# A four-stage trunk on one core: head 0's f and q together in the first stage, and a new order of loads and norms ahead of them

## The chip, the cores and the metric

The kernel runs on one core of a Trainium2 chip. The metric is device time in microseconds (us): the median of several executions of the same program. A separate execution was taken by the hardware profiler, and every row of the profile is from that one.

## The reference

One inference step of a two-layer decoder trunk, in float32, for 1024 prompt tokens and 8 sample tokens (T = 1032 columns), with shared weights:

```python
def hgrn2_mixer(h, s0, w_in, lb, g_norm, w_out):       # layer 0
    q, f, i, z = jnp.split(h @ w_in, [D_MODEL, 2 * D_MODEL, 2 * D_MODEL + D_INNER], axis=-1)
    q = jax.nn.silu(q)                                   # 8 heads of 128
    logf = jnp.logaddexp(jnp.log(lbh), jnp.log1p(-lbh) + jax.nn.log_sigmoid(f))
    k = -jnp.expm1(logf)
    o, S = hgrn2_chunkwise(q, k, i, logf, s0)            # gated linear recurrence
    return (rmsnorm(o, g_norm) * jax.nn.silu(z)) @ w_out, S

def trunk(x, p, ...):
    h = x
    for i in range(DEPTH):                               # DEPTH = 2; layer 1 is a chunked gMLP
        hn = rmsnorm(h, norm_mix[i])
        y = hgrn2_mixer(hn, ...) if i % 2 == 0 else chunk_mlp_mixer(hn, ...)
        h = h + y
        gate = jax.nn.sigmoid(rmsnorm(h, norm_ple[i]) @ w_ple_gate[i])
        h = h + gate * (p[i] @ w_ple_proj[i])            # D_MODEL 1024, p has 256 features
    return rmsnorm(h, norm_final), new_s, new_v
```

## The kernel before

**Tiling.** Features lie on the 128 partitions (D_MODEL is eight blocks, k or j = 0 to 7), tokens on the free axis in three chunks c = 0, 1, 2 of W = 384, 384 and 264 columns. A float32 product is made of three matmuls in a reduced format (`mm3`): each operand is split into a high part (a cast on ScalarE: `bh` or `ph` for activations, `whi` for weights) and a low part (source minus high part: `bl`, `pl`, `wlo`), and TensorE adds hi·hi, lo·hi and hi·lo in PSUM. A projection `proj` of one 128-wide block of weights for one chunk is eight such triples. In the profile's lines these are L228, L229 (needs the low part of the activation) and L230 (needs `wlo`).

**The first stage**, around which the change lies, in the order of TensorE:

1. Twelve matmuls on zeros as warm-up (`zo<-zr`).
2. `pple(0, ..., half 0)`: the first half of layer 0's p @ w_ple_proj, a fill of work while the first norm runs: for every chunk four output blocks m, each two triples; chunk 0, then 1, then 2. ScalarE copies each result out of PSUM (`pple_t`), and it is stored to DRAM.
3. `first_norm(c)` for each chunk, a process that is stepped on by ticks between the pieces of TensorE work. It squares x (`sq`, ScalarE, two blocks at a time), adds the squares in pairs (`sq<-sq`: VectorE for chunk 0, GpSimd for chunks 1 and 2), sums over partitions on TensorE (`pss<-ones,sq`), takes `rms_e` on VectorE and the power −1/2 on GpSimd (`rsq`), spreads that over the partitions by TensorE (`pbc<-ident,rsq`), scales x by it on VectorE (`scalar_tensor_tensor`, called STT below: `xs<-xs,g,pbc`) and splits the result: `bh` on ScalarE, `bl` on VectorE for odd j and on GpSimd for even j. `SQD` and `SDEL` are the ticks that a process waits ahead of its squares, its sum and its broadcast.
4. For each chunk `fk` and then `qq`: the projection of head 0's forget gate (weights `("a", 8)`), then of its query (`("a", 0)`). ScalarE takes sigmoids of the one (`f`, and k into `qk`) and of the other (`sg`), and VectorE makes q = ps·sg (into `qk`).
5. Two blocks of z (weights `("a", 32)`, `("a", 33)`, called z0 and z1 below), while VectorE and ScalarE form mixed tiles of the normed x for the next stage (`mix_x`: `xs<-xs,xs`, then `xzh` and `xzl`).

**What sets the order.** TensorE runs in program order, written by hand. On the other engines a scheduler orders by program order, data and priority: work under `tc.high_priority(offset=PRI)` goes ahead, and `tc.issue_after(x)` keeps an instruction behind x. The accumulators of `pple` and `proj` share three PSUM banks (tag `mm`), those of the sums one. Input and output transfers are issued by SyncE, whose queue holds eight transfers open at a time: each issue waits for the eighth before it.

`norm_proc` serves the first norm (`own=True`: x is scaled in place) and the later norms (`own=False`: into one of four `tmp` buffers), among these the ones ahead of the two gate products (`ps_proj` at 912 us and its like in layer 1), which run beside the last output products (`ps_o`, added to `h` on VectorE).

```python
            split(hh[:, j, :], hl[:, j, :], t[:, :w], V if j % 2 else G)
...
    for c in CH:
        fk(0, r0, wf, c)
        qq(0, r0, wq, c)
```

Of the kernel before, what the change touches and what calls it, by code (L numbers as in the profile page):

```python
# [80 lines left out]
def trunk_kernel(ctx, tc, xT, st, pT, nrm, wina, lbl, gna, wouta, winb, lng, lnb, lngr, lnbr,  # L81
# [27 lines left out]
    with ExitStack() as s:  # L109
        zp = pool(s, "warm")  # L110
        zps = pool(s, "warm_ps", space=PSUM)
        zf = zp.tile([P, 512], F32, name="zf")
# [2 lines left out]
        V.tensor_copy(zr, zf)
        zo = zps.tile([P, 512], F32, name="zo")
        for _ in range(NWARM):
            PE.matmul(zo, zr[:, :P], zr, start=True, stop=True)
# [174 lines left out]
    def norm_proc(sp, ssq, src, gi, hh, hl, c, d, own=False):  # L293
# [6 lines left out]
        w = W[c]  # L300
        for j in range(KT):
            t = src(j) if own else sp.tile([P, 384], F32, name="tmp", bufs=4)
            V.scalar_tensor_tensor(t[:, :w], src(j), g32[:, gi, j:j + 1], pbc[:, :w], ALU.mult, ALU.mult)
# [1440 lines left out]
```

## Time and profile before

| | |
|---|---|
| time, median of 3 runs | 1866.89 us (1864.61 to 1870.77) |
| profiled execution, its own time | 1863.58 us |
| its span, first to last instruction | 1861.6 us |
| mean granted TensorE clock | 0.995 |
| busy: TensorE / VectorE / ScalarE / GpSimd | 98% / 73% / 48% / 22% |
| DMA, mean over the span | 137 GB/s of HBM traffic |
| first stage: warm-up from 2.01 us, first `pple` 7.30, first f 21.92, z0 54.40 | |

A timeline row reads: start and length in us, engine, source line, operation, output and inputs, size on the array, shape, count; in brackets the idle time of the engine ahead of it and what ended that. Matmuls are pipelined: a row of 0.34 us follows its neighbour by 0.17 where nothing is waited for, so rates are taken from starts. PE is TensorE, DVE VectorE, ACT ScalarE, POOL GpSimd.

### The profile page before, as it was taken

The page shows a single profiled execution, that of the slowest core. Times are in us where ns is not written, and L with a number is a line of the kernel's source. Part 1 is how long each engine was busy: PE and PEld are TensorE (multiplying, and loading weights), DVE is VectorE, ACT ScalarE, POOL GpSimd, SP SyncE. Part 2 cuts the span into 40 slices and gives each one's busy share as a digit, 9 for nine tenths or more (in the row PEclk, how much of TensorE's full clock was granted, in tenths as well). Part 3 has the DMA queues.
Part 4 walks back from the last instruction along what each step waited for, and adds up shares of the span by engine and source line. Part 5 has one row for each costly group of instructions (what it writes and reads, how often), then busy time and mean ns, then how long its engine had stood idle before and what let it go on. Part 6 is the DMA issues. An engine that isn't in the chain of part 4 may idle for free.

```text
span 1861.6 us, 37133 instructions
## 1 busy us (share of the span) xinstructions
PE 1822.4 (98%) x14458; PEld 1788.6 (96%) x14458; DVE 1360.5 (73%) x2760; ACT 897.6 (48%) x1905; POOL 402.3 (22%) x407
## 2 busy tenths in 40 slices
PE   8999999999999999999999999999999999999997
PEld 7999999999999998999999999999999999999997
DVE  7766888889888875867756755577778877877744
ACT  7533366556656655344444544434443435444342
POOL 4000011111111110000323233354444552000222
PEclk9999999999999999999999999999999999999999
DMA  6233344345444355853244343323334546953223
GB/s 220 79 112 106 112 127 128 108 152 182 149 130 140 117 176 185 278 184 96 87 145 140 101 136 92 95 79 119 129 117 143 172 129 215 305 179 104 72 92 114
DMA packets 164560, 258.11 MB, mean 139 GB/s; under 512 B 16096, under 2 KB 136864, under 8 KB 163360
## 3 DMA queue, kind: packets, MB, share of 16 engines
q1 hardware_dynamic: 164384, 255.74, 43.5%
q8 instruction: 113, 1.85, 0.4%
q14 instruction: 63, 0.52, 0.1%
HBM read 182.88 MB, written 72.80 MB: 137 GB/s over the span
## 4 chain that ended last, share of the span: by engine, by line
PE 80%; DVE 10%; DMA 5%; issue 2%; POOL 1%; ACT 1%; SPq 0%; DVEq 0%; ACTq 0%; POOLq 0%
PE ps_proj L228 19%; PE ps_proj L230 18%; PE ps_proj L229 18%; PE ps_d L228 2%; PE ps_o L228 2%; PE ps_d L230 2%; PE ps_d L229 2%; PE ps_o L229 2%; PE ps_o L230 2%; DVE wlo L150 1%; PE psp L1526 1%; DMA vb<-vd 1%; PE pt_o L899 1%; PE pt_g L1408 1%; PE pC L807 1%
## 5 line engine op out<-in xcount | busy, mean ns | idle before, releaser
L228 PE MATMUL ps_proj<-bh,whi 128*128 128x264 f32 (+1 forms) x2248 | 719.2, 320 | 4.3 <-ACT u L493 1.3
L229 PE MATMUL ps_proj<-bl,whi 128*128 128x264 f32 (+1 forms) x2248 | 700.8, 312 | 5.4 <-DVE bl L224 2.7
L230 PE MATMUL ps_proj<-bh,wlo 128*128 128x264 f32 (+1 forms) x2248 | 700.9, 312 | 1.2 <-DVE wlo L150 1.2
L228 PEld LDWEIGHTS ps_proj<-bh,whi 128*128 128x128 f32 x2248 | 423.6, 188 | 12.3 <-issue 3.3
L229 PEld LDWEIGHTS ps_proj<-bl,whi 128*128 128x128 f32 x2248 | 424.1, 189 | 8.9 <-DVE bl L224 5.4
L230 PEld LDWEIGHTS ps_proj<-bh,wlo 128*128 128x128 f32 x2248 | 422.6, 188 | 2.1 <-DVE wlo L150 2.1
L150 DVE TENSOR_TENSOR wlo<-wstg,whi 128x1024 fp32r<-128x1024 f32 x148 | 183.7, 1241 | 109.4 <-ACT whi L149 109.1
L149 ACT CAST whi<-wstg 128x1024 fp32r<-128x1024 f32 x148 | 155.2, 1049 | 150.0 <-PE ps_proj L229 125.0
L149 ACT CAST shi<-ssum 128x512 fp32r<-128x512 f32 x152 | 94.1, 621 | 187.3 <-PE ps_proj L229 90.1
L150 DVE TENSOR_TENSOR slo<-ssum,shi 128x512 fp32r<-128x512 f32 x152 | 113.9, 751 | 9.2 <-ACT shi L149 8.8
L237 POOL TENSOR_TENSOR rsq<-rms_e,mhalf 128x3 f32<-128x3 f32 x15 | 17.8, 1187 | 368.1 <-DVE rms_e L282 368.1
L857 DVE TENSOR_TENSOR qk<-qk,t 128x384 f32<-128x384 f32 (+1 forms) x144 | 77.2, 540 | 12.0 <-PE pC L807 11.3
L228 PE MATMUL ps_proj<-xmh,shi 128*128 128x384 f32 x244 | 83.0, 340 | 1.9 <-ACT xmh L223 1.7
L229 PE MATMUL ps_proj<-xml,shi 128*128 128x384 f32 x244 | 81.9, 336 | 0.7 <-DVE xml L224 0.7
L230 PE MATMUL ps_proj<-xmh,slo 128*128 128x384 f32 x244 | 81.7, 335 | 0.0
L228 PE MATMUL ps_o<-bh,whi 128*128 128x384 f32 (+1 forms) x232 | 73.4, 316 | 0.0
L230 PE MATMUL ps_o<-bh,wlo 128*128 128x384 f32 (+1 forms) x232 | 72.7, 313 | 0.0
L229 PE MATMUL ps_o<-bl,whi 128*128 128x384 f32 (+1 forms) x232 | 72.7, 313 | 0.0
L1535 POOL TENSOR_TENSOR s<-s,u 128x384 f32<-128x384 f32 (+1 forms) x48 | 54.1, 1127 | 70.9 <-DVE s L1529 70.3
L1274 DVE TENSOR_TENSOR tmp<-tmp,pj 128x384 f32<-128x384 f32 (+1 forms) x48 | 25.6, 534 | 55.9 <-ACT tmp L1273 52.0
L237 POOL TENSOR_TENSOR rsq<-ss_e,mhalf 128x3 f32<-128x3 f32 (+2 forms) x32 | 28.4, 889 | 145.7 <-DVE ss_e L893 145.7
L264 POOL TENSOR_TENSOR ssq<-ssq,tmp 128x384 f32<-128x384 f32 (+1 forms) x36 | 34.3, 951 | 108.1 <-ACT tmp L263 108.1
(376 smaller groups left out, 4135.8 us busy)
## 6 DMA issues: line engine op xcount, KB each, us to landing
wstg<-in_wina SPq DMA_DIRECT2D x48, 512.0 KB, 3.8
wstg<-in_winb SPq DMA_DIRECT2D x48, 512.0 KB, 4.0
pj<-ppd SPq DMA_DIRECT2D x16, 516.0 KB, 4.9
S<-in_st SPq DMA_DIRECT2D x16, 512.0 KB, 5.4
vb<-vd SPq DMA_DIRECT2D x16, 512.0 KB, 4.8
out_so_s<-S SPq DMA_DIRECT2D x16, 512.0 KB, 3.5
wstg<-in_wouta SPq DMA_DIRECT2D x16, 512.0 KB, 4.2
wstg<-in_wgate SPq DMA_DIRECT2D x16, 512.0 KB, 3.7
```

The costliest lines, as they stand in the source:

```text
L149: A.copy(hi, src)
L150: V.tensor_tensor(lo, src, hi.bitcast(F32), ALU.subtract)
L228: PE.matmul(ps, wh, xh, start=first, stop=False, skip_group_check=more)
L229: PE.matmul(ps, wh, xl, start=False, stop=False, skip_group_check=more)
L230: PE.matmul(ps, wl, xh, start=False, stop=last, skip_group_check=more)
L237: G.tensor_tensor(y, e, mhalf[:, :n], ALU.pow)
L264: eng.tensor_tensor(ssq, ssq, sq[:, :w], ALU.add)
L807: PE.matmul(out(slice(row, row + kt.shape[1])), kt, qt, start=True, stop=True)
L857: V.tensor_tensor(lev, lev, t2.rearrange("p two (n o) -> p two n o", o=1).broadcast_to([P, 2, n, lv]), ALU.mult)
L899: PE.transpose(pt[:, m, :], on[:, m * P:(m + 1) * P], ident)
L1274: V.tensor_tensor(gt[:, :w], gt[:, :w], pj[:, OFF[c]:OFF[c] + w], ALU.mult)
L1535: G.tensor_tensor(s[:, :w], s[:, :w], us[mm, c][:, :w], ALU.mult)
```

## The change

- The warm-up's operand shrinks from 128x512 to 128x128; its moving side is one column read 512 times.
- Loads: the first weights (`("p", 0, 0)`) come in pieces of 256 and 768 columns, chunk 0's p in two halves between them; x of chunk 0 follows at once; p of chunks 1 and 2, each followed by the weights of f or q, stands behind chunk 0's x and the constants. q's weights are split during the fill (`load(2)` at i = 5).
- First norm: all low parts on VectorE, STT and low part alternating (STT j behind low part j − 2), at high priority; for chunks 1 and 2 no pair additions on GpSimd, TensorE sums eight rows in place of four (96 matmuls in place of 48 for each of them). `SQD` and `SDEL` are new. The `pple` copies of this half go to high priority.
- `proj2`: for chunks 0 and 1 f and q run k by k in two banks; chunk 2 stays f, then q.
- The later norms get `high_priority(offset=0)` around STT and split.

```diff
-SQD = (0, 6, 12)
+SQD = (0, 10, 14)
-SDEL = ((6, 3), (6, 2), (4, 2))
+SDEL = ((6, 2), (4, 1), (4, 1))
...
-        zr = zp.tile([P, 512], F32R, name="zr")
+        zr = zp.tile([P, P], F32R, name="zr")
-            PE.matmul(zo, zr[:, :P], zr, start=True, stop=True)
+            PE.matmul(zo, zr, zr[:, 0:1].broadcast_to([P, 512]), start=True, stop=True)
...
+        lows = []
         for j in range(KT):
             t = src(j) if own else sp.tile([P, 384], F32, name="tmp", bufs=4)
-            V.scalar_tensor_tensor(t[:, :w], src(j), g32[:, gi, j:j + 1], pbc[:, :w], ALU.mult, ALU.mult)
-            split(hh[:, j, :], hl[:, j, :], t[:, :w], V if j % 2 else G)
+            with tc.high_priority(offset=PRI if own else 0):
+                with tc.issue_after(lows[j - 2].ins) if own and j > 1 else ExitStack():
+                    V.scalar_tensor_tensor(t[:, :w], src(j), g32[:, gi, j:j + 1], pbc[:, :w], ALU.mult, ALU.mult)
+                split(hh[:, j, :], hl[:, j, :], t[:, :w], V if j % 2 or own else G)
+            lows.append(last["lo"])
...
-                with tc.high_priority(offset=PRI if l else 0):
+                with tc.high_priority(offset=0 if half and not l else PRI):
                     last["pple"] = A.copy(t, ps[:, :W[c]])
...
-    load(0)
+    loaded[0] = [t.rearrange("p k t -> p (k t)")[:, :1024] for t in (hh[2], hl[2])]
+    first_weights(0, 2 * P)
-    load_p(sp, 0, 0, ph, pl)
-    load_p(sp, 0, 1, ph, pl)
+    load_p(sp, 0, 0, ph, pl, single=True)
+    first_weights(2 * P, 1024)
     load_x(0)
...
+    load_p(sp, 0, 1, ph, pl)
+    fetch_weights(1)
     load_p(sp, 0, 2, ph, pl)
+    fetch_weights(2)
     load_x(1)
-    fetch_weights(1)
     load_x(2)
-    fetch_weights(2)
...
-            eng.tensor_tensor(sq[:, j, :], sq[:, j, :], sq[:, j + 1, :], ALU.add)
+            if not c:
+                V.tensor_tensor(sq[:, j, :], sq[:, j, :], sq[:, j + 1, :], ALU.add)
-    ... norm_proc(sp, [sq[:, j, :] for j in range(0, KT, 2)], ...
+    ... norm_proc(sp, [sq[:, j, :] for j in range(0, KT, 1 if c else 2)], ...
...
+    def proj2(w1, w2, c):
+        both = [(wt, pp.tile([P, 512], F32, name="ps_proj", tag="mm", bufs=3)) for wt in (w1, w2)]
+        for k in range(KT):
+            for (wh, wl), ps in both:
+                mm3(ps[:, :W[c]], blk(wh, k), blk(wl, k), hh[c][:, k, :], hl[c][:, k, :], k == 0, k == KT - 1)
+            if k in (1, 3, 5):
+                tk.tick()
+        return [ps for _, ps in both]
...
-        if i == 8:
-            with tc.issue_after(last["pple"].ins):
-                load(1)
+        if i == 5:
+            load(2)
...
     for c in CH:
-        fk(0, r0, wf, c)
-        qq(0, r0, wq, c)
+        pf, pq = proj2(wf, wq, c) if c < 2 else (None, None)
+        fk(0, r0, wf, c, pf)
+        qq(0, r0, wq, c, pq)
```

How instructions move is shown at three places. The number after a name's underscore tells one use of a buffer from another; `ps_proj_504` is chunk 0's f before, `ps_proj_563` its q, `ps_proj_436` and `ps_proj_437` the same two after, `ps_proj_644` chunk 1's f before; `xs1`, `bh1`, `bl1` are chunk 1's, `xs2`, `bl2` chunk 2's.

First, ScalarE where chunk 0's f and q leave PSUM, before:

```order
L223 CAST bh1_137<-xs1_155 128x384 x2
L605 ACT_TABLE_LOAD
L605 ACTIVATE f_529<-ps_proj_504 128x384
L606 ACTIVATE qk_530<-ps_proj_504 128x384
L607 ACTIVATE f_529<-f_529,lb_182 128x384
L618 ACTIVATE sg_588<-ps_proj_563 128x384
L608 ACTIVATE qk_530<-qk_530,lb_182 128x384
L223 CAST bh1_137<-xs1_155 128x384 x6
```

and after:

```order
L223 CAST bh1_137<-xs1_155 128x384 x2
L632 ACT_TABLE_LOAD
L632 ACTIVATE f_620<-ps_proj_436 128x384
L223 CAST bh1_137<-xs1_155 128x384 x2
L633 ACTIVATE qk_621<-ps_proj_436 128x384
L645 ACTIVATE sg_626<-ps_proj_437 128x384
L634 ACTIVATE f_620<-f_620,lb_180 128x384
L223 CAST bh1_137<-xs1_155 128x384
```

Two casts of chunk 1 now stand between the two sigmoids that read f's bank (L605 and L606 before are L632 and L633 after).

Second, VectorE in the norms of chunks 1 and 2, before:

```order
L303 SCALAR_TENSOR_TENSOR xs1_155<-xs1_155,g32_72,pbc_535 128x384 x4
L619 TENSOR_TENSOR qk_530<-ps_proj_563,sg_588 128x384
L282 TENSOR_SCALAR rms_e_640<-pss_591 128x3
L644 TENSOR_SCALAR gn16_813<-gn16_813 128x2
L425 TENSOR_TENSOR xs0_154<-xs1_155,xs0_154 128x384
L224 TENSOR_TENSOR bl1_140<-xs1_155,bh1_137 128x384
```

and after:

```order
L306 SCALAR_TENSOR_TENSOR xs1_155<-xs1_155,g32_72,pbc_580 128x384
L224 TENSOR_TENSOR bl1_140<-xs1_155,bh1_137 128x384
L646 TENSOR_TENSOR qk_621<-ps_proj_437,sg_626 128x384
L224 TENSOR_TENSOR bl1_140<-xs1_155,bh1_137 128x384
L282 TENSOR_SCALAR rms_e_740<-pss_643 128x3
L435 TENSOR_TENSOR xs1_155<-xs1_155 128x384 x2
L306 SCALAR_TENSOR_TENSOR xs2_156<-xs2_156,g32_72,pbc_756 128x264 x2
```

Chunk 2's `rms_e` stood ahead of chunk 1's last three low parts (of VectorE's four) and stands behind all eight now.

Third, VectorE in the norm ahead of layer 0's gate product (`tmp`, `bh0` and `bl0` are its chunk 0; `h2_6` and `h2_7` are the last additions of the output products), before:

```order
L303 SCALAR_TENSOR_TENSOR tmp_12321<-h0_3_10573,g32_72,pbc_12305 128x384
L224 TENSOR_TENSOR bl0_12231<-tmp_12313,bh0_12228 128x384
L1150 TENSOR_TENSOR h2_6_10592<-h2_6_10592,ps_o_12345 128x264
L282 TENSOR_SCALAR rms_e_12383<-pss_12370 128x3
L303 SCALAR_TENSOR_TENSOR tmp_12325<-h0_4_10574,g32_72,pbc_12305 128x384
L150 TENSOR_TENSOR wlo_12167<-wstg_12164,whi_12166 128x1024
L224 TENSOR_TENSOR bl0_12231<-tmp_12321,bh0_12228 128x384
L303 SCALAR_TENSOR_TENSOR tmp_12329<-h0_5_10575,g32_72,pbc_12305 128x384
L1150 TENSOR_TENSOR h2_7_10593<-h2_7_10593,ps_o_12391 128x264
```

and after:

```order
L306 SCALAR_TENSOR_TENSOR tmp_12413<-h0_3_10665,g32_72,pbc_12397 128x384
L306 SCALAR_TENSOR_TENSOR tmp_12417<-h0_4_10666,g32_72,pbc_12397 128x384
L1179 TENSOR_TENSOR h2_6_10684<-h2_6_10684,ps_o_12437 128x264
L282 TENSOR_SCALAR rms_e_12475<-pss_12462 128x3
L150 TENSOR_TENSOR wlo_12259<-wstg_12256,whi_12258 128x1024
L306 SCALAR_TENSOR_TENSOR tmp_12421<-h0_5_10667,g32_72,pbc_12397 128x384
L306 SCALAR_TENSOR_TENSOR tmp_12425<-h0_6_10668,g32_72,pbc_12397 128x384
L1179 TENSOR_TENSOR h2_7_10685<-h2_7_10685,ps_o_12483 128x264
L224 TENSOR_TENSOR bl0_12323<-tmp_12405,bh0_12320 128x384
L224 TENSOR_TENSOR bl0_12323<-tmp_12413,bh0_12320 128x384
```

The low parts of blocks 1 and 3 stood ahead of the addition to `h2_7` and stand behind it now. In layer 1's gate norm the same rows move in the same way.

More of the change, by code (lines that the diff above doesn't have):

```diff
@@ L318, in proj, with load_p @@
         return ps
-    def load_p(ap, l, c, ph, pl, behind=None, to=None):
+    def load_p(ap, l, c, ph, pl, behind=None, to=None, single=False):
         stg = ap.tile([P, 2, W[c]], F32, name=f"pstg{c}", bufs=1)
+        if single:
+            ph[c], pl[c] = [ap.tile([P, 2, W[c]], F32R, name=f"p{x}{c}") for x in "hl"]
+            for k in range(2):
+                load_split(ph[c][:, k], pl[c][:, k], pT[l][:, k, OFF[c]:OFF[c] + W[c]], stg[:, k])
+            return
         nc.sync.dma_start(stg, pT[l][:, :, OFF[c]:OFF[c] + W[c]])
@@ L558, in load_x, with first_weights @@
             nc.sync.dma_start(xs[c][:, j:j + 2, :], xT[:, j:j + 2, OFF[c]:OFF[c] + W[c]])
-    load(0)
+    loaded[0] = [t.rearrange("p k t -> p (k t)")[:, :1024] for t in (hh[2], hl[2])]
+    w0stg = wp.tile([P, 1024], F32, name="wstg")
+    def first_weights(a, b):
+        load_split(loaded[0][0][:, a:b], loaded[0][1][:, a:b], wproj[0, 0][:, a:b], w0stg[:, a:b])
     ph, pl = [None] * 3, [None] * 3
-    load_p(sp, 0, 0, ph, pl)
-    load_p(sp, 0, 1, ph, pl)
+    first_weights(0, 2 * P)
+    load_p(sp, 0, 0, ph, pl, single=True)
+    first_weights(2 * P, 1024)
     load_x(0)
@@ L581, in first_norm @@
         sq = sp.tile([P, KT, 384], F32, name="sq0", bufs=2)[:, :, :W[c]]
-        eng = V if c == 0 else G
         for j in range(0, KT, 2):
@@ L586, in first_norm @@
                 A.activation(sq[:, j:j + 2, :], xs[c][:, j:j + 2, :], AF.Square)
-            eng.tensor_tensor(sq[:, j, :], sq[:, j, :], sq[:, j + 1, :], ALU.add)
-        yield from norm_proc(sp, [sq[:, j, :] for j in range(0, KT, 2)], lambda j: xs[c][:, j, :], 0, hh[c], hl[c], c, SDEL[c], True)
+            if not c:
+                V.tensor_tensor(sq[:, j, :], sq[:, j, :], sq[:, j + 1, :], ALU.add)
+        yield from norm_proc(sp, [sq[:, j, :] for j in range(0, KT, 1 if c else 2)], lambda j: xs[c][:, j, :], 0,
+                             hh[c], hl[c], c, SDEL[c], True)
     V.tensor_tensor(lb[:, 1, :], lb[:, 0, :], lb[:, 0, :], ALU.subtract)
@@ L611, in fk, with qq @@
         tk.tick()
-    def qq(h, r, wt, c):
+    def qq(h, r, wt, c, ps=None):
         w = W[c]
-        ps = proj(wt, hh[c], hl[c], c)
+        ps = ps or proj(wt, hh[c], hl[c], c)
         sg = fq.tile([P, 384], F32, name="sg", bufs=2)
@@ L628, in trunk_kernel @@
     for i, _ in enumerate(fill):
-        if i == 8:
-            with tc.issue_after(last["pple"].ins):
-                load(1)
+        if i == 5:
+            load(2)
         tk.tick()
     r0 = new_head()
-    wf, wq = take("a", 8), take("a", 0)
+    wf, wq = take("a", 8), loaded[2]
     for c in CH:
-        fk(0, r0, wf, c)
-        qq(0, r0, wq, c)
+        pf, pq = proj2(wf, wq, c) if c < 2 else (None, None)
+        fk(0, r0, wf, c, pf)
+        if c == 2:
+            take("a", 0)
+        qq(0, r0, wq, c, pq)
     assert not tk.procs
```

6 lines of the change are left out of this document (3 added, 3 removed).

## The prediction

> **What bounds the kernel now.** I read the page's head first, then the busy time by stretches of the stage that the change touches, then what TensorE waited for there (from 0 to 56 us), then the timelines engine by engine.
>
> ```profile
> span 1861.6 us, 37133 instructions
> PE 1822.4 (98%) x14458; PEld 1788.6 (96%) x14458; DVE 1360.5 (73%) x2760; ACT 897.6 (48%) x1905; POOL 402.3 (22%) x407
> ...
> 21.90:31.40 9.50, 6.40 (x40) 4.65 (x31) 8.97 (x10) 6.16 (x13) 9.17 (x8) 1.00 0.84 279
> 31.40:43.80 12.40, 11.02 (x154) 9.79 (x152) 10.94 (x21) 7.53 (x16) 5.35 (x6) 1.00 0.15 46
> 43.80:54.40 10.60, 10.31 (x75) 10.09 (x75) 10.60 (x22) 8.26 (x21) 3.41 (x4) 1.00 0.00 0
> 54.40:77.40 23.00, 22.82 (x147) 22.51 (x146) 20.11 (x37) 12.50 (x27) 0.00 (x0) 1.00 0.34 108
> ...
> PE ps_proj L229 <- POOL bl L224: 2.5, 3, 1.1
> PE zo L118 <- DVE zr L115: 2.0, 1, 2.0
> PE ps_proj L229 <- DVE bl L224: 2.0, 3, 1.1
> PE ps_proj L230 <- DVE wlo L150: 0.5, 2, 0.3
> ```
>
> PE is busy 98% of the span, so the change can win only what PE loses where it reaches. After each stretch stand its length and the busy time of PE, PEld, DVE, ACT and POOL, then PE's granted clock, the DMA share and GB/s. PE is busy 6.40 of 9.50 us while chunk 0's f runs; POOL (9.17) and DVE (8.97) are full there, and the waits are for low parts from either. In the stretch 43.80 to 54.40 DVE is never idle (10.60 of 10.60), and from 54.40 PE runs full. So the limit is the norm's elementwise work, DVE's above all; whatever makes z0 start earlier or later moves everything behind it.
>
> ```profile
> 2.01 5.49 PE L118 MATMUL zo<-zr 128*128 128x512 f32 x12 [2.01 <-DVE zr L115]
> 7.30 0.52 PE L228 MATMUL ps_pple<-ph,whi 128*128 128x384 f32 x1
> ...
> 21.92 0.44 PE L228 MATMUL ps_proj<-bh,whi 128*128 128x384 f32 x1
> 35.77 0.98 PE L279 MATMUL pss<-ones,sq 128*32 128x1 f32 x96
> 36.68 0.44 PE L228 MATMUL ps_proj<-bh,whi 128*128 128x384 f32 x1
> 43.19 0.73 PE L290 MATMUL pbc<-ident,rsq 128*128 128x128 f32 x6
> 43.78 0.42 PE L228 MATMUL ps_proj<-bh,whi 128*128 128x384 f32 x1
> 48.02 0.28 PE L228 MATMUL ps_proj<-bh,whi 128*128 128x264 f32 x1
> 49.11 0.28 PE L228 MATMUL ps_proj<-bh,whi 128*128 128x264 f32 x1
> 49.47 0.28 PE L228 MATMUL ps_proj<-bh,whi 128*128 128x264 f32 x1
> 54.40 0.34 PE L228 MATMUL ps_proj<-bh,whi 128*128 128x384 f32 x1
> 55.08 0.44 PE L230 MATMUL ps_proj<-bh,wlo 128*128 128x384 f32 x1 [0.18 <-DVE wlo L150]
> ```
>
> Prices: chunk 1's q, eight triples, takes 43.78 to 48.02, so 0.53 us a triple of 384 columns (0.52 taken); one of 264 takes 49.11 to 49.47, 0.36. Chunk 2's sum, right behind chunk 0's q, takes 35.77 to 36.68, 0.91; a broadcast 43.19 to 43.78, 0.59. From f's start at 21.92 to 54.40 are 32.48 us: 32 triples of 0.52 and 16 of 0.36 make 22.4, one sum (0.91; chunk 1's is earlier) and two broadcasts 2.1. The other 8.0 are waits, the most that the reordering of f and q can win.
>
> ```profile
> 1.53 0.43 DVE L115 CAST zr<-zf 128x512 fp32r<-128x512 f32 x1
> 18.94 2.71 DVE L303 SCALAR_TENSOR_TENSOR xs<-xs,g,pbc 128x384 f32<-128x384 f32 x5 [3.49 <-PE pbc L290]
> 22.77 2.58 DVE L224 TENSOR_TENSOR bl<-xs,bh 128x384 fp32r<-128x384 f32 x2
> ...
> 44.01 2.08 DVE L303 SCALAR_TENSOR_TENSOR xs<-xs,g,pbc 128x264 f32<-128x264 f32 x5
> 48.82 0.42 DVE L224 TENSOR_TENSOR bl<-xs,bh 128x264 fp32r<-128x264 f32 x1
> 53.82 1.21 DVE L150 TENSOR_TENSOR wlo<-wstg,whi 128x1024 fp32r<-128x1024 f32 x1
> 57.37 2.89 DVE L224 TENSOR_TENSOR xzl<-xs,xzh 128x384 fp32r<-128x384 f32 x6
> ...
> 6.00 0.83 ACT L326 CAST ph<-pstg 128x768 fp32r<-128x768 f32 x1 [0.28 <-DMA pstg<-in_pT]
> 8.45 0.85 ACT L586 ACTIVATE sq<-xs 128x768 f32<-128x768 f32 x1 [0.19 <-DMA xs<-in_xT]
> 9.51 0.85 ACT L586 ACTIVATE sq<-xs 128x768 f32<-128x768 f32 x1 [0.22 <-DMA xs<-in_xT]
> ...
> 33.42 1.28 ACT L605 ACT_TABLE_LOAD   x1
> 34.71 0.49 ACT L605 ACTIVATE f<-ps_proj 128x384 f32<-128x384 f32 x1
> 36.94 2.58 ACT L223 CAST bh<-xs 128x384 fp32r<-128x384 f32 x6
> 15.53 0.85 POOL L237 TENSOR_TENSOR rsq<-rms_e,mhalf 128x3 f32<-128x3 f32 x1 [15.02 <-DVE rms_e L282]
> ```
>
> An STT takes 2.71 / 5 = 0.54. A low part takes 2.89 / 6 = 0.48 where POOL stands still (`xzl`), but 2.58 / 2 = 1.29 at 22.77, while POOL makes low parts itself. The Trainium skill (SBUF — State Buffer, "SBUF: two separate sides") says that VectorE with two SBUF inputs and GpSimd shut each other out of a shared port for a whole instruction; those 1.29 us agree.
>
> **The change part by part.** The walk below carries these prices through the new order.
>
> *Warm-up and first products.* The cast of 512 columns takes 0.43, the memset ahead of it about as much; a quarter of the columns saves at most 0.65. The first weights and p come in pieces, so the first `pple` starts at about 6.7 in place of 7.30 (bounds: 7.3, if the halved p is no earlier, and 6.6). Chunk 0 is eight triples, 4.2: PE is through at 10.9.
>
> *p of chunk 1 behind x of chunk 0.* Two squares that wait for DMA start 1.06 apart, so one such piece (128x768 words) lands in 1.06. With chunk 1's p out of their way, x's four pieces land 1.06 earlier, the last at 10.6 by that pace; constants (mostly two tables of 128x128, 0.4) and p (1.06) follow, 12.0. Ahead of p's cast in ACT's queue stand the last square (0.85), one `pple` copy and the exponential of `lb`, which itself waits for DVE: I put the cast's end at 13.3 (0.83 long) and `pl`, 0.95, at 14.3. q's weights are split in the fill (1.21 on DVE), in the 3.49 in which DVE was idle ahead of 18.94: nothing, or 1.2 later STTs if that idle time goes. The `pple` copies' priority costs nothing: PE waited for no bank, and a copy pushes a square back by less than 0.5. SyncE's queue holds nothing else back: the weights of f and q come behind p, and f starts at 22 us. So PE, which had no wait here, stands still from 10.9 to 13.3 at least and 15.2 at most, if the constants' chain on DVE holds `pl` up: 3.4 taken, of which the earlier start had given 0.6. Behind it in PE's order: four triples (2.1) to 16.4, chunk 0's sum (0.9) to 17.3, four triples to 19.4, the broadcast to 20.0. So STT begins at 20.0 (bounds 18.9, as before, and 20.9) where it began at 18.94. Chunk 2's eight small triples, 2.9, end at 22.9, and f and q begin 1.0 later than f did.
>
> *Low parts on DVE, f and q k by k, chunk 0.* DVE needs 0.54 + 0.48 = 1.02 a block, PE two triples, 1.04: they keep pace as long as POOL touches nothing, and its pair additions are gone. Those cost PE instead one doubled sum, 1.8 (0.9 more for each of chunks 1 and 2). 22.9 + 8.3 + 1.8 + 0.6 = 33.6. Before, q of chunk 0 ended at 35.77: 2.1 won.
>
> *Chunk 1.* q needs a third bank, which is f's of chunk 0 until both its sigmoids are done. f ends at 33.1, the table load takes 1.28, the sigmoid 0.4, and now two casts (2.58 / 6 = 0.43 each) stand ahead of the second sigmoid: 36.1. PE has one triple of f to do, so it waits 2.1 (bounds 1.2, were the table loaded early, and 2.5). Seven blocks follow: to 39.6 with the sum's 1.8, to 41.7 with two more. Chunk 2's `rms_e` now stands behind all of chunk 1's low parts on DVE, so `rsq` (0.85) is done at 42.4 and PE, at its broadcast, waits 0.7 (0 to 1.5). With 0.6 and four blocks: 47.3.
>
> *Chunk 2*, f then q as before. DVE has eight STTs of 2.08 / 5 = 0.42 and eight low parts of 0.42 (before: half of them), and ACT makes the high parts between chunk 1's sigmoids and scalings, 2.6 in all. The last low part comes at 51.0, f ends at 51.4, q eight triples later: 54.3.
>
> *z0* needs `wlo` (1.21) behind some seven mixing steps and low parts of 0.48 on DVE: 51.0 + 3.4 + 1.2 = 55.6, at the worst 56.9. Before, PE's first triple with it was at 55.08. So the end of the stage moves by +0.5 to +1.8; **+1.1** is taken. Everything won by pairing f and q is given back by DVE's sum (8 of 1.02 each for two chunks, 8 × 0.84, the mixing) from a later STT.
>
> *The gate norms.* Here the low parts are pushed back, in two places.
>
> ```profile
> 909.15 0.55 DVE L224 TENSOR_TENSOR bl<-tmp,bh 128x384 fp32r<-128x384 f32 x1
> 912.87 0.43 DVE L1150 TENSOR_TENSOR h<-h,ps_o 128x264 f32<-128x264 f32 x1
> ...
> 912.67 0.34 PE L228 MATMUL ps_proj<-bh,whi 128*128 128x384 f32 x1
> 918.26 0.44 PE L229 MATMUL ps_proj<-bl,whi 128*128 128x384 f32 x1 [0.35 <-DVE bl L224]
> ```
>
> PE starts the gate product at 912.67 and wants block 1's low part 0.53 later. That was made at 909.15; it now stands behind the addition to `h2_7`, which begins at 912.87 because it waits for PE, and behind an STT that waits for a free `tmp`, thus for POOL's low parts: about 915.0, a wait of 1.75. But the product already waited at 918.26 for its last low part, which comes no later than before by more than 0.5, since DVE has the same work to do. So +0.5 each (bounds 0 and 1.75), **+1.0** for two.
>
> Sum: +1.1 + 1.0 = +2.1 on the profiled execution's 1863.58 us. That lies 3.3 below the median of the runs, 1866.89; against the median the forecast is **1869.0**.
>
> **The rivals.** *B, the waits don't bite.* p of chunk 1 is cast as soon as it lands, the second sigmoid and `rms_e` find free slots. PE then goes from 22.9 by 22.4, two doubled sums of 1.8 and two broadcasts to 50.1; DVE's own sum from STT at 20.0 is 8.2 + 8.2 + 6.7 + mixing and `wlo` 6.6, 49.7. z0 began at 54.40 and lost 0.34 to its `wlo`, so that is −4.6; −6.6 if STT also begins at 18. For it: each wait hangs on a queue position worked out by hand. Against: three have to vanish together. 1860 to 1862.
>
> *C, the other side: the gate norms decide.* Two places with three chunks each; if each chunk loses the whole 1.75, that is 10.5: 1877.4. For it: the low parts of all chunks are pushed back alike, with the work of both DVE and POOL between. Against: chunks 1 and 2 have a chunk's product (4 us) of lead. It is slower by over 0.3% from about 0.75 us a chunk, given the stage's +1.1.
>
> *D, the clock.* The new gap of 3.4 us falls where PE has just warmed up. In the trace the granted clock is 1.00 in all four stretches, whose longest wait is 1.1 us, so no gap of this length is shown. If the clock were halved for about as long again, work of 3.4 us would take 1.7 longer at once: 1870.7. For this the Trainium skill (TensorE: Matmul & The Clock Gate, "What's actually happening") speaks: after an idle window of about 3.4 us the array falls to half its clock. By it the sum is +3.8; without it, +2.1.
>
> **How the numbers follow.** A difference of 0.3%, 5.6 us, is about what can be told from no change in this kernel: the band is 1861.3 to 1872.5. Forecast (both terms small): 0.62, from +0 to +5, thus 1867 to 1872. B: 0.18, half of it beyond the band. C: 0.10, nearly all beyond. D: 0.10, inside. Faster 0.10 (half of B and a little), same 0.80, slower 0.10. The range reaches from B's better half to half of C: 1861 to 1875.
>
> **What would show it.** Right: a gap of 2.4 to 4.3 us on PE ahead of chunk 1's first `pple`, ended by `ph` or `pl`; STT at about 20; f and q of chunk 0 without waits to 33.6; a wait of about 2 us ahead of q of chunk 1, ended by the second sigmoid; one for `rsq` ahead of chunk 2's broadcast; z0's `wlo` triple at 55.5 to 56.9; and waits for `bl` early in both gate products. The prediction is wrong if DVE's low parts take 0.5 but the ones on ACT they wait for are late, or if PE works through f and q of all chunks by 50: then z0 moves up by 4 or more. The clock at 11 to 18 us decides D.

## The result: 0.85% slower, and the profile after

The changed kernel takes 1881.87 us (median of 6 runs, 1880.24 to 1886.60) beside 1867.76 for the kernel before on the same chip: ratio 1.0085, 95% interval 1.0066 to 1.0104. The forecast was 1869.0, the range 1861 to 1875. The profiled execution took 1881.57 us, its span:

```profile
span 1879.8 us, 37502 instructions
PE 1829.7 (97%) x14650; PEld 1796.0 (96%) x14650; DVE 1361.7 (72%) x2774; ACT 899.4 (48%) x1907; POOL 380.9 (20%) x387
```

TensorE has 192 rows more, the doubled sums: each of the two has 48 more matmuls, and a matmul of a sum stands in the profile as two rows. What it waited for in the first 60 us, total, times, longest:

```profile
PE pss L279 <- issue: 4.4, 2, 2.6
PE ps_pple L228 <- ACT ph L335: 2.3, 1, 2.3
PE ps_proj L228 <- ACT qk L633: 2.1, 1, 2.1
...
PE ps_pple L229 <- DVE pl L336: 0.6, 1, 0.6
```

The waits of f and q for low parts are gone, as the change intends. The largest entry is one that the prediction has no word for: "issue", time in which the engine waited for nothing that the profile shows, and it lies in the middle of the two long sums. The timeline of TensorE (`bh` and `bl` in rows of `ps_pple` are the first weights, which lie in buffers of that name now):

```profile
14.35 0.44 PE L228 MATMUL ps_pple<-ph,bh 128*128 128x384 f32 x1 [2.31 <-ACT ph L335]
15.34 0.69 PE L229 MATMUL ps_pple<-pl,bh 128*128 128x384 f32 x1 [0.55 <-DVE pl L336]
...
21.90 0.83 PE L290 MATMUL pbc<-ident,rsq 128*128 128x128 f32 x6
25.48 0.34 PE L228 MATMUL ps_proj<-bh,whi 128*128 128x384 f32 x1
30.22 1.34 PE L279 MATMUL pss<-ones,sq 128*32 128x1 f32 x141
33.33 0.61 PE L279 MATMUL pss<-ones,sq 128*32 128x1 f32 x51 [1.77 <-issue]
...
43.17 0.44 PE L228 MATMUL ps_proj<-bh,whi 128*128 128x384 f32 x1 [2.07 <-ACT qk L633]
44.97 1.53 PE L279 MATMUL pss<-ones,sq 128*32 128x1 f32 x163
49.08 0.59 PE L279 MATMUL pss<-ones,sq 128*32 128x1 f32 x29 [2.58 <-issue]
67.73 0.44 PE L230 MATMUL ps_proj<-bh,wlo 128*128 128x384 f32 x1 [0.61 <-DVE wlo L150]
```

A sum of 192 rows breaks off after 141, the next after 163. And z0's first triple with its `wlo`, at 55.08 before, stands at 67.73: +12.65 us, so most of the loss is made in this stage. The busy time by stretches (after the five engines stand the granted clock, the DMA share and GB/s) shows what each gap costs besides itself:

```profile
11.90:14.90 3.00, 0.58 (x2) 0.19 (x1) 2.07 (x9) 2.50 (x5) 0.00 (x0) 0.99 1.04 399
...
14.82:18.23 3.41, 2.89 (x9) 2.89 (x10) 2.31 (x3) 1.61 (x3) 0.00 (x0) 0.50 1.05 375
18.23:35.30 17.07, 15.09 (x366) 14.15 (x365) 10.12 (x19) 11.97 (x24) 1.71 (x2) 1.00 0.84 275
35.30:38.72 3.42, 3.42 (x15) 3.42 (x14) 0.51 (x1) 0.00 (x0) 0.00 (x0) 0.50 0.01 2
38.72:48.95 10.23, 5.71 (x186) 5.04 (x184) 9.18 (x20) 7.32 (x14) 0.00 (x0) 1.00 0.01 2
48.95:55.78 6.83, 6.70 (x50) 6.69 (x51) 1.95 (x6) 0.33 (x1) 1.09 (x1) 0.50 0.01 2
55.78:67.70 11.92, 10.85 (x72) 9.90 (x71) 11.21 (x27) 9.13 (x22) 0.00 (x0) 1.00 0.01 1
```

Three times, behind the gap ahead of chunk 1's p and behind each broken sum, the granted clock is exactly 0.50, for 3.41, 3.42 and 6.83 us. TensorE is busy for 13.0 us of these, and at half clock half of that is lost: 6.5 us. The Trainium skill (TensorE: Matmul & The Clock Gate, "What's actually happening") gives just two clocks, full and half, and a window of about 3.4 us; the 0.50 and the lengths 3.4 and 6.8 agree.

The spells start 20.48 and 13.65 us apart, six and four times 3.41. So it is in all traces, this one, the one of before and those of the experiments: a spell of half clock that ends before the program does lasts a whole multiple of 3.41 us, and within one trace any two start a whole multiple of 3.41 us apart. The clock is thus set anew in fixed steps of 3.41 us, and what a gap costs depends on where it falls in these steps and not on its length alone: the wait of 2.07 us for the bank lies in the stretch from 38.72 to 48.95, which has full clock throughout.

Later in the program the offset between the two traces is 11.1 to 11.5 us from 720 to 930 us, 13.1 at 960, 15.1 at 1700 and 16.1 at 1790. Where the instructions are the same the offset drifts too (that of e6_before_long_sums, below, whose later stages are those of the kernel before, by 4.2 us between 960 and 1500 us), and the one profiled execution of before lies 2 to 4 us under its medians, so only the steps at the gate products (950, 1775 to 1790) are taken up below.

### The profile page after: what moved, and what is told of

Same layout as the page of the kernel before. It is cut to its first block, busy times and chain, and to the rows that moved or that the text cites. A ratio compares the mean times of both kernels' runs of the same rounds, so it can differ in the third digit from the quotient of the medians.

```text
span 1879.8 us, 37502 instructions
## 1 busy us (share of the span) xinstructions
PE 1829.7 (97%) x14650; PEld 1796.0 (96%) x14650; DVE 1361.7 (72%) x2774; ACT 899.4 (48%) x1907; POOL 380.9 (20%) x387
## 4 chain that ended last, share of the span: by engine, by line
PE 80%; DVE 10%; DMA 4%; ACT 2%; issue 2%; POOL 1%; SPq 0%; DVEq 0%; ACTq 0%; POOLq 0%
PE ps_proj L228 19%; PE ps_proj L230 18%; PE ps_proj L229 18%; PE ps_d L228 2%; PE ps_d L230 2%; PE ps_d L229 2%; PE ps_o L228 2%; PE ps_o L229 2%; PE ps_o L230 2%; PE psp L1555 1%; DVE wlo L150 1%; DVE bl L224 1%; PE pt_o L928 1%; PE pt_g L1437 1%; PE pC L836 1%
## 5 line engine op out<-in xcount | busy, mean ns | idle before, releaser
L886 DVE TENSOR_TENSOR qk<-qk,t 128x384 f32<-128x384 f32 (+1 forms) x144 | 77.4, 541 | 12.1 <-PE pC L836 11.2
L1303 DVE TENSOR_TENSOR tmp<-tmp,pj 128x384 f32<-128x384 f32 (+1 forms) x48 | 26.0, 545 | 56.1 <-ACT tmp L1302 49.7
L237 POOL TENSOR_TENSOR rsq<-ss_e,mhalf 128x3 f32<-128x3 f32 (+2 forms) x32 | 28.7, 898 | 144.4 <-DVE ss_e L922 138.4
```

The lines of the kernel that those rows point to most:

```text
L237: G.tensor_tensor(y, e, mhalf[:, :n], ALU.pow)
L886: V.tensor_tensor(lev, lev, t2.rearrange("p two (n o) -> p two n o", o=1).broadcast_to([P, 2, n, lv]), ALU.mult)
L1303: V.tensor_tensor(gt[:, :w], gt[:, :w], pj[:, OFF[c]:OFF[c] + w], ALU.mult)
```

## The experiments

Two theories were set against each other. **S and D:** the long sums outrun the supply of TensorE's instructions, and every gap of 2 to 3 us, whatever its cause, lowers the clock behind it. **The rival:** VectorE's chain sets the end of the stage, and TensorE merely waits in other places.

### Half of the long sums

```diff
-range(0, KT, 1 if c else 2)]
+range(0, KT, 2)]
```

> The changed kernel, but TensorE sums only the four even rows of squares for chunks 1 and 2 (48 matmuls in place of 96 each; the odd rows' squares are left out of the norm). In the changed kernel each long sum breaks off in the middle: 1.8 us after 141 rows of 192, 2.6 us after 163, with no releaser named, and each is followed by some 3 to 5 us of matmuls at about half pace. Theory S (a burst of so many tiny matmuls outruns the supply of TensorE's instructions, and the pause then lowers the clock): both pauses go, so do the slow stretches behind them, the last broadcast of the stage comes 8 us earlier or more, about 1872 against 1881. Rival N (the norm's elementwise work sets the end of the stage, the pauses are only where TensorE happens to wait): the pauses turn into waits for rsq or low parts, the end moves by under 3 us. Rival Q (the pauses are any refill, tied to a place in the program and not to the number of sums): pauses of the same length appear elsewhere in the first 60 us.

Measured: 1871.07 us, ratio 1.0028 (1.0018 to 1.0039). TensorE's timeline:

```profile
31.16 0.98 PE L279 MATMUL pss<-ones,sq 128*32 128x1 f32 x96
43.07 1.02 PE L279 MATMUL pss<-ones,sq 128*32 128x1 f32 x96
```

Both sums run through; at 80 us the offset to the kernel before is 4.6 in place of 12.7. That is 8.1 us for 192 rows whose own time is 1.8: the long sums carry two thirds of the loss in this stage. The gap for p is still there, and with it a clock of 0.50 from 15.9 to 22.7 us; the bank wait (2.0) has one from 39.8 to 43.2 behind it, where the same wait had none in the changed kernel.

### Chunk 1's p ahead of chunk 0's x

```diff
+    load_p(sp, 0, 1, ph, pl)
     load_x(0)
...
-    load_p(sp, 0, 1, ph, pl)
```

> The changed kernel with chunk 1's p loaded ahead of chunk 0's x instead of behind the constants. Theory (a gap of about 2.9 us ahead of chunk 1's first product, then 1.4 us lost at half clock): the gap of 2.3 + 0.55 us and the slow matmuls from 15.3 to 18.1 us vanish, x and the first scaling's loads come 1.06 us later, net 2.5 to 4 us earlier at the first scaling and 2 to 4 us on the whole, about 1878. Rival (the late x takes it back, the sum and the broadcast of chunk 0 are then the wait): under 1 us on the whole.

Measured: 1881.55 us, 1.0079 (1.0066 to 1.0092): nothing told apart from the changed kernel. The rival came nearer, though not by its wait. The first scaling did come 5 us earlier (its broadcast at 16.93), and then:

```profile
28.72 0.69 PE L230 MATMUL ps_proj<-bh,wlo 128*128 128x384 f32 x1 [2.76 <-DVE wlo L150]
33.76 1.78 PE L279 MATMUL pss<-ones,sq 128*32 128x1 f32 x192
45.06 1.53 PE L279 MATMUL pss<-ones,sq 128*32 128x1 f32 x162
49.11 0.60 PE L279 MATMUL pss<-ones,sq 128*32 128x1 f32 x30 [2.52 <-issue]
```

VectorE's scalings and low parts, at high priority and now early, stood ahead of the split of q's weights: a new wait of 2.76, with half clock from 28.7 to 32.1, after another such spell from 21.8 to 25.2 behind waits of 0.72 and 1.63 for chunk 2's p. Chunk 1's sum ran through here, so a long sum does not always break.

### Chunk 1's f and q apart

```diff
-proj2(wf, wq, c) if c < 2 else (None, None)
+proj2(wf, wq, c) if c < 1 else (None, None)
```

> The changed kernel, but chunk 1's f and q run one after the other; only chunk 0's go k by k. Theory (q of chunk 1 waits 2.07 us for f's bank of chunk 0, behind the table load and two casts): the wait goes; f of chunk 1 has to wait for low parts instead where TensorE outruns VectorE (two triples were 1.04 us a block, one is 0.52, VectorE makes 1.0 a block), so some 2 us come back as waits for bl: change of the whole between -2 and +1 us, 1880 to 1883. Rival (the bank wait is what starts the following slow clock stretch): -4 us, 1878.

Measured: 1879.45, 1.0066 (1.0053 to 1.0079). The wait for the bank is gone, waits for low parts of 0.9 us in all came for it, and the stage ends 2.7 us earlier (65.01). Pauses in the sums remain, 3.2 us in place of 4.4; so some 1.2 of the 2.7 come from shorter pauses, and the rest is about what the bank's 2.07 less the new 0.9 would give. Neither theory's extreme.

### The old order in the gate norms

```diff
-            with tc.high_priority(offset=PRI if own else 0):
+            with tc.high_priority(offset=PRI) if own else ExitStack():
```

> The changed kernel with the old order of scaling and split in the two gate norms (no priority there). In the changed kernel those places moved the end by nearly 0 at each first gate product (offset 11.2 to 11.5 us against the kernel before around 800 and 918 us), but a wait of 1.1 us for a weight's low part stands at 951 us that the kernel before lacks, and the offset there grows to 13.1. Theory G0 (the gate norms cost nothing): within 1 us of the changed kernel, 1881 to 1883. Rival G2 (they cost that wait at both places): 2 to 3 us less, 1879.

Measured: 1878.03, 1.0063 (1.0050 to 1.0076); this interval overlaps the changed kernel's, but the traces say G2. The offset to the kernel before stays at 11.3 from 800 to 960 us and at 12.5 from 1700 to the end, where the changed kernel goes from 11.2 to 13.1 and from 15.1 to 16.1: 2.9 us for the two places. In the changed kernel the wait for a low part that was forecast is there, at the start of the gate product, but by that product's end it has moved the offset by only 0.2. Most of the price is paid 26 us later:

```profile
925.26 0.44 PE L229 MATMUL ps_proj<-bl,whi 128*128 128x384 f32 x1 [0.51 <-DVE bl L224]
...
951.78 0.44 PE L230 MATMUL ps_proj<-bh,wlo 128*128 128x384 f32 x1 [1.14 <-DVE wlo L150]
```

VectorE carries the same work in another order, and the next weights' low part comes out late (in layer 1 by a wait of 0.34).

### The long sums in two bursts

```diff
-        yield d[0]
+        yield d[0] - 1 if half else d[0]      # half: chunks 1 and 2 of the first norm
+        if half:
+            with tc.high_priority(offset=PRI):
+                pss = norm_sum(sp, ssq, c, None, range(4))      # rows 0 to 3; rows 4 to 7 a tick later
+            yield 1
...
```

> The changed kernel with the same 96 matmuls in each long sum, but in two bursts of 48, the first one tick (two blocks of f and q) earlier. Theory S (a burst of more than some 140 rows outruns the supply of TensorE's instructions): no pause without a releaser in the first 60 us, the slow stretches behind the two sums go or shrink, 6 to 9 us less than the changed kernel, about 1874. Rival C (it is the number of instructions in the stage that the supply can't keep up with, wherever they stand): the pauses stay, about 4 us in all, and the time is that of the changed kernel within 2 us.

The bursts share columns of one bank, and a column then holds only a part of the sum, here and in e8_all; instructions and operands are those of the whole. Measured: 1876.90, 1.0057 (1.0040 to 1.0073). TensorE:

```profile
31.30 0.55 PE L281 MATMUL pss<-ones,sq 128*32 128x1 f32 x45
32.77 0.60 PE L281 MATMUL pss<-ones,sq 128*32 128x1 f32 x51 [0.93 <-issue]
```

Chunk 2's sum no longer breaks, chunk 1's does for 0.93, and the stage's end is 5.3 us better than in the changed kernel, a little under what S expected. But S as it was written, that a burst of more than some 140 rows runs dry, does not hold: this burst has 96 rows and breaks. Note where it breaks: 96 + 45 = row 141, the same row as in the changed kernel, though another 12 matmuls now stand between the bursts. They were moved, not added: the break is tied to a count of TensorE's instructions. The next three experiments bear that out.

### The long sums alone, in the kernel before

```diff
-            eng.tensor_tensor(sq[:, j, :], sq[:, j, :], sq[:, j + 1, :], ALU.add)
+            if not c:
+                eng.tensor_tensor(sq[:, j, :], sq[:, j, :], sq[:, j + 1, :], ALU.add)
```

and eight rows summed for chunks 1 and 2.

> The kernel before with one part of the change: chunks 1 and 2 sum eight rows on TensorE (96 matmuls in place of 48) and GpSimd adds no pairs. Theory S: 1.8 us more of sums, and a pause of 1.5 to 2.5 us in chunk 1's sum, which follows 14 us of dense products, with a slow stretch behind it; chunk 2's, behind products that wait for low parts, none. Against that GpSimd's four additions ahead of chunk 0's low parts go. Net +1 to +5 us, 1867 to 1871. Rival (GpSimd's additions were what held the low parts up): 2 us or more faster.

Measured: 1873.82, 1.0039 (1.0026 to 1.0051), above the expected +1 to +5, and chunk 2's sum, which was expected to run through, breaks too.

```profile
21.77 1.54 PE L279 MATMUL pss<-ones,sq 128*32 128x1 f32 x164
27.06 0.60 PE L279 MATMUL pss<-ones,sq 128*32 128x1 f32 x28 [3.74 <-issue]
38.54 1.63 PE L279 MATMUL pss<-ones,sq 128*32 128x1 f32 x174
42.09 0.43 PE L279 MATMUL pss<-ones,sq 128*32 128x1 f32 x18 [1.92 <-issue]
```

Without anything else of the change, both sums break, and each has nearly 7 us of half clock behind it; the stage ends 5.4 us later, although GpSimd's eight additions are gone. This one part turns the tuned kernel into a slower one.

Counting rows from one break to the next: here 28 of the sum, 48 of f and q, 6 of the broadcast, 174 of the sum make 256; in the changed kernel 51 of the sum, 24 of f and q, 6 of the broadcast, 12 of f and q and 163 of the sum, again 256. A row is a matmul and its weight load, so the breaks are 512 instructions apart. Counted from the first matmul, every pause without a releaser inside a sum, in all the traces of this document, comes after 350 or 351 rows or after 606 or 607. It is such a place that breaks a sum, if the sum happens to lie across it, and not the length of the sum.

### The gap ahead of chunk 1's p filled

```diff
+        if i == 3:
+            zo2 = pp.tile([P, 512], F32, name="pss", tag="po", bufs=1)
+            for _ in range(14):
+                PE.matmul(zo2[:, :W[0]], loaded[0][0][:, :P], ph[0][:, 0, :], start=True, stop=True)
```

> The changed kernel with 14 extra matmuls of 384 columns (2.4 us, results unused) in the gap ahead of chunk 1's first product, where TensorE waits for p. Theory D (idleness lowers the clock): the granted clock stays 1.00 from 11 to 22 us, the gap itself stays 2 to 3 us, and what follows comes 1.7 us earlier than in the changed kernel, 3.4 where the low clock lasted 6.8 us. Rival (the clock falls for another reason, power or a fixed time after the start): it is low there all the same. On the whole 1.5 to 3.5 us less, 1878 to 1880.

Measured: 1871.73, 1.0028 (1.0016 to 1.0041), 10 us better than the changed kernel by work that nobody uses; more than expected.

```profile
11.90:14.90 3.00, 2.71 (x16) 2.40 (x14) 2.13 (x8) 2.49 (x5) 0.00 (x0) 1.00 1.04 396
14.90:18.20 3.30, 3.08 (x108) 2.81 (x108) 2.02 (x3) 2.15 (x5) 0.00 (x0) 1.00 1.05 374
...
11.84 2.59 PE L659 MATMUL pss<-ph,bh 128*128 128x384 f32 x14
28.71 1.78 PE L279 MATMUL pss<-ones,sq 128*32 128x1 f32 x192
40.02 1.41 PE L279 MATMUL pss<-ones,sq 128*32 128x1 f32 x148
43.01 0.55 PE L279 MATMUL pss<-ones,sq 128*32 128x1 f32 x44 [1.58 <-issue]
```

The same 3 us that had 0.58 of work have 2.71, p is as late as before, and the clock stays at 1.00 (the changed kernel: 0.50). So the idle time lowers the clock, D. By luck the 14 matmuls also did something for the sums: chunk 2's breaks 15 rows earlier (148 for 163), much as a count of instructions demands, and chunk 1's not at all.

Why not, the instruction queue's transfers show, each a packet of 16 KB; here of the changed kernel in the stretches 30.8 to 30.9 and 46.6 to 46.7 us, and then of this one in 26.7 to 26.8 and 40.6 to 40.7:

```profile
q8 instruction: 1, 0.02, 55.8%
q8 instruction: 1, 0.02, 58.0%
...
q8 instruction: 1, 0.02, 69.7%
q8 instruction: 1, 0.02, 59.9%
```

In the changed kernel the sums go on at 33.33 and 49.08, 2.5 and 2.4 us behind the packets at 30.8 and 46.7; here chunk 2's at 43.01, 2.4 behind 40.6, and chunk 1's, which came to its row 351 at 29.8, had its packet at 26.8, in time. In e6_before_long_sums the packets at 24.4 and 39.7 are followed by 27.06 and 42.09. The second packet of a trace goes with row 351 and the fourth with row 607, wherever a sum lies across such a row: a broken sum goes on 2.3 to 2.9 us behind it, and a sum that comes to such a row 2.6 us or more behind its packet runs through. That holds for chunk 1's sum in e2_p1_first (2.75 us) and for the kernel before, whose chunk 2 has row 351 in a sum of 96 at 35.9, with its packet at 24.5. The Trainium skill (Runtime: NRT & Kernel Launch, "Instruction fetch mechanics") says that each engine's instructions come in blocks of 16 KiB, 256 instructions, and that the cost of a boundary is mostly hidden: the packets agree, two of them to each 512 instructions between breaks, but in a burst of 9 ns rows the cost is 0.3 to 3.7 us. Why a packet sometimes leaves early (26.8) and sometimes only at the break (46.7, with the data queues at 2 GB/s) isn't settled.

### A quarter of the instructions for the long sums

```diff
-                for b in range(0, P, 32):
-                    PE.matmul(pss[b:b + 32, i:i + 1], t[:, o + b:o + b + 32], ...
+                n = P if len(parts) == KT else 32
+                for b in range(0, P, n):
+                    PE.matmul(pss[b:b + n, i:i + 1], t[:, o + b:o + b + n], ...
```

> The changed kernel with each long sum made of 24 matmuls with 128 columns of squares as the stationary side in place of 96 with 32: the same additions, a quarter of the instructions. Theory S (the supply of instructions breaks off when so many tiny ones are run in so short a time): no pause without a releaser in the two sums, and the slow stretches behind them go; a sum takes 1.8 to 4.5 us (48 rows at 0.04 us, if loads of 32 columns cost a quarter of one of 128, to 0.1 us, as in the broadcasts). 1873 to 1879. Rival F (TensorE pauses at those places in the program for another reason than the rate, a refill that is due there anyway): a pause of 1.5 us or more stays at the same distance in instructions, somewhere in the products.

Measured: 1891.86, 1.0137 (1.0115 to 1.0159). No pause anywhere: rows 351 and 607 lie in products of 384 columns now, and F, which asks for a pause there too, falls. But the price was out of my range:

```profile
30.28 5.68 PE L280 MATMUL pss<-ones,sq 128*128 128x1 f32 x48
47.50 10.23 PE L280 MATMUL pss<-ones,sq 128*128 128x1 f32 x48
...
35.29:38.70 3.41, 3.41 (x13) 3.41 (x13) 1.09 (x3) 0.00 (x0) 1.10 (x1) 0.50 0.01 2
45.53:62.59 17.06, 17.06 (x74) 17.06 (x72) 5.33 (x12) 2.65 (x6) 1.09 (x1) 0.50 0.00 1
```

A row of 128 columns takes 0.12 us in the first sum, some twelve times one of 32. And the clock falls to 0.50 at 35.29 behind a sum in which TensorE was busy without a gap: matmuls that move one column do not hold it up. Behind the bank wait (2.0 us) it falls again at 45.53, and it stays down through the whole second sum.

### The large stalls taken away together

The edits of the old gate order and of the two bursts, and these:

```diff
         for j in range(0, KT, 2):                      # load_x(0)
+            if j == 4 and mid:
+                mid()                                   # load_p(sp, 0, 1, ph, pl)
...
     A.activation(lb[:, 1, :], lb[:, 1, :], AF.Exp)
+    A.activation(sgw, lb[:, 1, :], AF.Sigmoid)
...
-        with tc.high_priority(offset=PRI if ... else 0):
+        with tc.high_priority(offset=PRI if ... or n in (1, 2) else 0):     # weights of f and q
...
+            with tc.high_priority(offset=PRI) if ap is sp0 and c else ExitStack():
                 A.copy(ph[c], stg)
```

> The changed kernel with every stall that the profile named taken away in turn: sums in two bursts of 48, chunk 1's p between the halves of chunk 0's x and its cast at high priority, the sigmoid table loaded early (a sigmoid of eight columns behind the exponential), the splits of f's and q's weights at high priority, and the old order in the two gate norms. If the stalls and the low clock explain the loss, the first stage's end (the first product of z with the weight's low part, 55.1 before, 67.7 in the changed kernel) comes at 51 to 55 us, and the whole at 1862 to 1867, the kernel before's time or up to 0.25% less. Rival (VectorE's low parts are the limit and the pairing of f and q gains nothing): 56 to 58, 1868 to 1870.

Measured: 1867.45, 1.0011 (1.0001 to 1.0022). In the first 60 us no stretch is below full clock, and z0's `wlo` triple is back where it was:

```profile
18.20:31.30 13.10, 11.85 (x252) 10.89 (x252) 10.63 (x20) 11.08 (x23) 1.10 (x1) 1.00 0.94 309
31.30:42.70 11.40, 10.12 (x241) 9.18 (x239) 9.64 (x21) 6.10 (x13) 1.23 (x1) 1.00 0.17 54
42.70:55.30 12.60, 11.51 (x78) 10.57 (x76) 12.05 (x28) 9.45 (x22) 0.00 (x0) 1.00 0.01 1
55.34 0.44 PE L230 MATMUL ps_proj<-bh,wlo 128*128 128x384 f32 x1 [0.64 <-DVE wlo L150]
```

Taken together, the stalls, what they do to the clock, and the gate norms thus account for all but 2 of the 14 us; this run does not share them out. Small stalls remain: the sums still pause at rows 351 and 607, for 0.29 and 0.38 us. What remains of the change itself, an end at 55.34 against 55.08, is no gain: between the 51 to 55 of the theory and the 56 to 58 of its rival. DVE works 12.05 of the last 12.60 us, as it did before: from chunk 2's scalings on its work sets the end.

### Two attempts at a version that beats both, and f and q apart again

```diff
-    fetch_weights(1)
     load_p(sp, 0, 2, ph, pl)
+    fetch_weights(1)
...
+                at = i + 4 * (j // 4) if js else i      # the second burst's columns
...
+        if js:
+            V.tensor_tensor(e, e, pss[:, 4:7], ALU.add)
```

> As e8_all, but the two bursts of a long sum go to columns of their own and are added on VectorE, chunk 2's p is loaded ahead of f's weights, and z0's weights are split at high priority too. The first stage's end, with neither a pause nor a low clock, is then set by VectorE's chain from the first scaling on: 53.5 to 55.5 us for the first product with z0's wlo (55.1 before). Whole: 1864 to 1867, the kernel before's time within 0.2%. If pairing f and q really gains once nothing is in its way: 51 to 53, 1861 to 1863.

Measured: 1869.46, 1.0011 (0.9997 to 1.0026); the offset at 80 us is 4.3, no better than e8_all's 0.3, because chunk 1's sum broke again (1.28 us) and chunk 2's broadcast waited 2.4 us for `rsq`. The low clock followed both times. Chunk 2's sum came to its row 606 2.6 us behind its packet and ran through.

```diff
-            if not c:
-                V.tensor_tensor(sq[:, j, :], sq[:, j, :], sq[:, j + 1, :], ALU.add)
+            if c != 1:
+                (G if c else V).tensor_tensor(sq[:, j, :], sq[:, j, :], sq[:, j + 1, :], ALU.add)
```

> As e10_mended, but chunk 2's squares are added in pairs on GpSimd again and summed by 48 matmuls; its additions fall where VectorE waits for chunk 1's broadcast. Theory S: no pause in chunk 2's sum (there was none in e10), 0.9 us less of sums on TensorE, the wait for rsq (2.4 us in e10) 1 to 2 us: z0's first product with its wlo at 53.5 to 57 us, the whole at 1864 to 1868. Rival: GpSimd's additions hold up VectorE's low parts as in the kernel before: no better than e10.

Measured: 1864.59 beside 1866.84, ratio 0.9985 (0.9972 to 0.9997): the lowest of all and just below the kernel before. Yet its profiled execution has a worse stage (the offset at 80 us is 3.6, and the broadcast waits longer), so where 2 us would come from isn't shown:

```profile
43.62 1.45 PE L298 MATMUL pbc<-ident,rsq 128*128 128x128 f32 x6 [3.19 <-POOL rsq L237]
```

```diff
-proj2(wf, wq, c) if c < 2 else (None, None)
+proj2(wf, wq, c) if c < 0 else (None, None)
```

> As e11_gpsimd_c2, but f and q of every chunk run one after the other. If pairing f and q is what lets TensorE keep pace with VectorE's 1.1 us a block, f of chunks 0 and 1 now waits for low parts, some 0.5 us a block (8 blocks, 4 us a chunk, of which the q behind it, already supplied, gives most back only if VectorE is not the limit): 2 to 6 us later than e11 at z0. If VectorE's chain sets the end of the stage whatever TensorE does: within 1.5 us of e11.

Measured: 1867.82, 1.0001 (0.9990 to 1.0011); the stage ends within 0.6 us of e11's (offset 3.0 against 3.6). TensorE waits often but briefly, and the clock does not fall in this stage:

```profile
PE ps_proj L229 <- DVE bl L224: 2.6, 12, 0.3
```

What VectorE waited for from 16 to 60 us, in e11 (two lines) and then here:

```profile
DVE xs L320 <- PE pbc L298: 4.9, 3, 2.3
DVE bl L224 <- ACT bh L223: 2.5, 2, 2.3
...
DVE xs L320 <- PE pbc L298: 3.1, 2, 2.6
```

Pairing f and q, the change's leading idea, shows no gain at the stage's end. That it has none isn't shown: e11 carries a pause of 0.69 us, a wait of 3.19 and 6.8 us of half clock that this run is without, and VectorE, whose work fills the end of the stage, waits in both for TensorE's broadcasts. The runs' medians differ by 3 us in e11's favour, with intervals that overlap.

## Why the prediction was wrong

**The step that failed** is the term "one doubled sum, 1.8" (and "0.9 more for each"). Its price came from a row of 48 matmuls and was doubled. The second 96 rows did cost 0.9 each; but in the burst TensorE ran out of instructions, 1.77 and 2.58 us, so that the two sums took 3.65 and 4.63 us from their start to the next product, and the clock fell behind them, which lost 1.7 and 3.3 us more. No row of before had a burst beyond 96, so the price had no upper bound from the trace, and I gave it none.

**Rival D was not a rival but part of the forecast case.** I gave the low clock 0.10, once, at 1.7 us. It came three times and cost 6.5. The forecast itself held a gap of 3.4 us ahead of chunk 1's p, the very gap that D speaks of, and two more waits, and yet its sum has no term for the clock. The filled gap shows that this low clock comes of the idle time. It also takes less idle time than I assumed: 2.31 and 0.55 us with one matmul between. Luck has a part in it, since the same wait for the bank was followed by half clock in e1_half_sums, e4_gate_order and e9_wide_sums, and not in the changed kernel, e2_p1_first and e7_keep_warm.

Term by term:

- Warm-up and first products: 6.7 predicted, 5.67 measured; but the second piece of the first weights came late, waits of 1.11 and 0.37 that I had not foreseen, and chunk 0 ended at 11.9 for 10.9.
- The gap for chunk 1's p: 3.4 predicted, 2.31 + 0.55 measured. Right in mechanism (the cast behind squares and the exponential) and in size; then some 1.5 of low clock on top. STT at 22.77 for 20.0.
- f and q of chunk 0 without a wait for low parts: right. 33.6 predicted, 40.4 measured, of which 1.77 is the pause, 1.7 the low clock and 2.6 the later start.
- The bank behind two casts: 2.1 predicted, 2.07 measured. Removing it (chunk 1 apart) gave 2.7 at z0, 1.2 of it by shorter pauses.
- The broadcast of chunk 2 waiting for `rsq`: hidden by the pause; without the pause it appears (0.9 in e8_all).
- z0's `wlo` triple: 55.6 predicted, 67.73 measured. The difference of 12.1 is, as near as the trace lets it be added up, 4.35 of pauses, 6.5 of low clock and about 1 for the weights' second piece. Without the stalls it stood at 55.34.
- The gate norms: +1.0 predicted as a wait for low parts, 2.9 measured in the traces, 0.2% of the time by the medians. The forecast wait came (0.51 in each gate product) and cost 0.2 to 0.3 each; missed was the next `wlo`, 1.14 and 0.34, which carries most of the price. So the mechanism was right for the small part, the sign right, and the size within its outer bound of 3.5.
- Rival B (the waits don't bite, −5): not what the changed kernel did, and even with the large stalls away the stage ended where it did before. VectorE's own sum had allowed it (49.7 without idle time), but it idles at each broadcast, 2.31 and 1.16 in e8_all, since the sums come late in TensorE's order.

## To carry to other kernels

A gap on TensorE of 2 us or more can be priced twice: its own length, and half of the 3.4 or 6.8 us at half clock behind it. Whether the second price falls due depends on where the gap lies in the clock's steps of 3.41 us, so it belongs in a forecast as a term with a chance. Filling a gap with matmuls that nobody uses can be worth more than shortening it. Runs of tiny matmuls need a bound of their own, since their cost per row in one burst says nothing on how fast instructions arrive in another: look for "issue" in the waits and for the instruction queue's packets. And when a chain on another engine fills the end of a stage, a new order of TensorE's work may gain nothing there, while a stall that it puts ahead of that chain's input counts in full.

## What the runs showed of the hardware

- TensorE's supply of instructions can break off at places 256 rows (matmul and weight load) apart, and a burst of rows of 9 ns that met such a place too soon behind its 16 KB packet of the instruction queue stood still for 0.29 to 3.74 us, until 2.3 to 2.9 us after that packet.
- The granted clock went to 0.50 for 3.41 us or a whole multiple of it, in fixed steps of 3.41 us. It did so behind some gaps of 1.3 to 3.7 us and not behind others (2.07 us in the changed kernel), and also behind 5.7 us of gapless matmuls that move one column each.
- A weight load of 128 columns with one moving column took 0.12 us a row in float32 at full clock and 0.21 at half, one of 32 columns 0.009.
